# Hybrid S5 / RG-LRU / GLA block with ConvFFN: a new order for the first norm, the projection stream and one FFN operand, and a last scaling on VectorE with stores in two queues

## The chip, the cores and the metric

The kernel runs on one core of one Trainium2 chip. The metric is the device time of one execution in microseconds (us), the median of the runs. Engines are called PE (TensorE), DVE (VectorE), ACT (ScalarE), POOL (GpSimd) and SP (SyncE); PEld is the loading of weights into PE. Each engine works through its own queue in order. L12 is line 12 of the kernel's file.

## The reference, cut to what matters

One layer on 1024 latent tokens of width 1024, with a prefix of 256 context tokens. All of it is fp32.

```python
mod = split((silu(c) @ ada_w + ada_b), 6)
u  = rms_norm(h, ln1_g) * (1 + mod[1]) + mod[0]          # latent; uc likewise for the context
z  = u @ w_in                                            # 5408 columns: s5, lru x, lru gate, q, k, v, g, z, 3 gates
s5  = s5_branch(z);  lru = rglru_branch(z);  gla = gla_branch(z)
m   = sum(sigmoid(gate[i]) * (y[i] @ w_br[i]) for i in range(3))
h   = h + mod[2] * (m @ w_out)
u   = rms_norm(h, ln2_g) * (1 + mod[4]) + mod[3]
gate, val = split(dwconv3(u @ w_up), 2)                  # 2 x 2816 columns
h   = h + mod[5] * ((silu(gate) * val) @ w_down)
out = rms_norm(h, final_g)
```

## The kernel before

**Products.** Channels lie on the 128 partitions and tokens on the free axis. Each fp32 matrix is split into a high part (a cast on ACT, L220, tiles ending in h) and a low part (the rest, a subtraction on DVE or POOL, L221, tiles ending in l); a product is three matmuls, high by high, high by low, low by high. A matmul is 128x512 unless said otherwise.

**Start.** The list `START` is an order written out by hand for every engine; each entry calls one small step. `x` loads a tile of the input and `sq` squares it on ACT (L391), `sa` adds the squares (L395; on DVE, but on POOL for the three entries of `ONPOOL`), `rs`, `re`, `rp`, `rb`, `rc` make the norm's factor (sums by PE, an addition on DVE, a power on POOL, a broadcast by PE, a copy on ACT). `a` loads one of the 8 pieces of a row of `ada_w` (SP), `ar` multiplies the 8 pieces (L316, 64 matmuls), `at`, `ac`, `am` bring the row into columns (DVE copy, PE, three DVE operations L365 to L367). `un`, `u`, `ul` make the operand `u` (DVE L320, ACT L323, DVE), `g`, `gh`, `gl` load and split the first weights, `m1`, `m2` are the first products (PE L434, L435, L441). The second argument is the half of the tokens, except for `a`, `ar` and the others on `ada_w`, whose first argument is the row.

**Stream.** `proj_stream` is a generator that yields the rest of the input projection matmul by matmul; `fill(us)` draws from it until a budget is spent, at 0.216 us a matmul, and `F(name)` takes the budget from the table `FILL`. So PE works on the projection while the recurrent branches keep DVE and ACT busy. Its weights come in the order of the list `wsrc`, over SP, with two raw buffers (wr) and three buffers of split weights (wh, wl). Each block of 1024 tokens is 48 matmuls and ends in a copy or an activation on ACT; `out_rows` (L577 to 581) copies and stores a block, `v_steps` makes rows of v for the context (copy L746), `z_steps` the decay's input (L703 to 718, its psum bank mb the one that L746 empties). These run beside the RG-LRU (`L971` to `L1005`); S5 follows (L1164 to L1264), then its GLU, then the four GLA heads.

**GLA heads and the end of the stream.** For each head `decays`, `keys` and `rest` run on DVE and ACT (L1303 to L1339); `transposed` (PE L1347) transposes the decayed keys that `keys` has made (DVE L1323). Head 0 has the budget `gtr` ahead of it. At the end of head 3 `scaled` broadcasts the norm (PE L279), scales on DVE and stores to `yosp` through SP; what is left of the stream is drawn by `fill(1e9)`. Then the four stored outputs are read back (`yr`, two buffers, L1549), split into `y0h`, `y0l` to `y3h`, `y3l` (ACT L220, DVE L221), and multiplied with w_br (PE L290 to L292).

**FFN up.** The products run as a scheme with seven instead of eight block products: operands `T1` to `T4` and `B11`, `B21`, `B22`, each a high and a low part of four 128x512 tiles. For the first two pairs of columns, `q[0]` and `q[1]`, the operands are made at the same time, in an order written by hand (`norm_order`): `hi(t, k)` and `lo(t, k)` make the parts of operand t (5 is B22), `sub` the differences, `units` the products by T1, T2, T3, `p3` the product by B22 (the scheme's third product), `p4` that by T4. `z57` (L1688, L1689) adds two products on DVE and so frees a psum bank for `p4`. `nxt` is the third pair.

**The end.** `last_out` broadcasts the last norm by PE, copies it to SBUF on ACT (L2188), scales eight tiles, six on DVE from psum (L2193) and two on POOL from the copy (L2191), and stores each through SP (L2194). It runs for three stretches of tokens; the last is tokens 256 to 511.

Of the kernel before, what the change touches and what calls it, by code (L numbers as in the profile page):

```python
# [20 lines left out]
KT = 8  # L21
# [16 lines left out]
def _parts(v, bits, n):  # L38
    out = []
    for _ in range(n):  # L40
# [69 lines left out]
def tile_kernel(tc, I, out, dbg=None):  # L110
# [154 lines left out]
    def t0(shape, tag, bufs=1):  # L265
        return p0_.tile(list(shape), F32, name=nm("t0"), tag=tag, bufs=bufs)
# [41 lines left out]
        SY.dma_start(w, (I["ada01"][r] if r < 4 else I["ada25"][r - 4])[:, k * 512:(k + 1) * 512])  # L308
        ada.setdefault(r, []).append(w)

    def ada_rows(r, p):


        for k, w in enumerate(ada.pop(r)):
            for j in range(4):
                PE.matmul(p[32 * j:32 * j + 32], c32[:, k], w[:, j * 128:(j + 1) * 128],  # L316
                          start=(k == 0), stop=(k == KT - 1), skip_group_check=True)
# [13 lines left out]
    class Start:  # L331
# [65 lines left out]
        @staticmethod
        def rs(j):
# [1935 lines left out]
```

## Time and profile before

| | us |
|---|---|
| median of 3 runs | 1577.93 (1577.77 to 1577.96) |
| the profiled execution, its own time | 1578.69 |
| span of the profiled execution, first to last instruction | 1576.6 |
| busy in the span: PE, PEld, DVE, ACT, POOL | 1513.6, 1248.9, 1096.1, 772.3, 414.6 |

Mean granted TensorE clock 0.985 of full speed; DMA 126 GB/s on average. The stages on the span's clock: start 0 to 72, stream with RG-LRU 140 to 235, S5 to 475, GLU and heads to 745, merge of the branches to 815, w_out and norm to 917, FFN up to 1410, FFN down to 1565, last norm to 1576.6. The profile is read by its page (busy time of each engine), by the list of waits (what an engine waited for, summed by line), by windows (busy time of each engine in a stretch) and by the timeline (single instructions with start and duration, the idle time before one in square brackets with what ended it). A busy PE is not PE at its peak.

### The profile page before, as it was taken

The numbers are of one execution on the slowest core, as the hardware profiler recorded it, in microseconds if no ns is written. First come the engines' busy times: TensorE is split into PE (matmuls) and PEld (weight loads), VectorE is DVE, ScalarE is ACT, GpSimd is POOL, SyncE is SP. The second block draws the span as 40 slices with busy tenths as digits, with TensorE's granted clock in tenths as the row PEclk, the third lists the DMA queues.
The fourth block names the chain that finished last, engine by engine and source line by source line (L and its number), as shares of the span: only waits on it lengthen the run. The fifth ranks groups of instructions, "written<-read, shape, count | busy, mean of one in ns | idle before, by whom it ended". The sixth has DMA issues, their size and how long they took to land. (4 is left out here: it accounts for less than half of the span.)

```text
span 1576.6 us, 21571 instructions
## 1 busy us (share of the span) xinstructions
PE 1513.6 (96%) x8144; PEld 1248.9 (79%) x8144; DVE 1096.1 (70%) x1645; ACT 772.3 (49%) x1223; POOL 414.6 (26%) x266
## 2 busy tenths in 40 slices
PE   5999989999996999999999989999999999999997
PEld 4788768877885888888888867778888888878887
DVE  3624379999858434642451899888888888899962
ACT  4523776785534543441332565444444444544661
POOL 2313210011124222222236335333333333000032
PEclk9999999999998999999999999999999999999998
DMA  9764533332224244131574411222222223964303
GB/s 327 256 213 132 187 129 105 117 101 59 59 67 134 77 135 148 70 88 63 172 239 145 141 60 54 94 81 80 81 81 83 93 92 109 371 240 141 101 20 107
DMA packets 93865, 199.04 MB, mean 126 GB/s; under 512 B 13505, under 2 KB 34881, under 8 KB 93633
## 3 DMA queue, kind: packets, MB, share of 16 engines
q1 hardware_dynamic: 82048, 181.75, 34.3%
q10 hardware_dynamic: 11712, 15.91, 2.9%
q8 instruction: 64, 1.05, 0.3%
q14 instruction: 41, 0.33, 0.1%
HBM read 159.11 MB, written 38.52 MB: 125 GB/s over the span
## 5 line engine op out<-in xcount | busy, mean ns | idle before, releaser
L221 POOL TENSOR_TENSOR wl<-wr,wh 128x1024 fp32r<-128x1024 f32 (+1 forms) x78 | 164.2, 2105 | 477.1 <-ACT wh L220 432.8
L220 ACT CAST wh<-wr 128x1024 fp32r<-128x1024 f32 (+2 forms) x87 | 77.1, 891 | 146.2 <-issue 41.3
L221 POOL TENSOR_TENSOR wp<-tmp,wp 128x512 fp32r<-128x512 f32 x44 | 75.2, 1726 | 217.6 <-ACT wp L220 217.6
L534 PE MATMUL ma<-uh,wh 128*128 128x512 f32 x272 | 116.9, 430 | 0.7 <-ACT pt L809 0.7
L534 PE MATMUL mb<-uh,wh 128*128 128x512 f32 x272 | 106.7, 392 | 0.0
L536 PE MATMUL ma<-ul,wh 128*128 128x512 f32 x272 | 106.7, 392 | 0.0
L536 PE MATMUL mb<-ul,wh 128*128 128x512 f32 x272 | 106.7, 392 | 0.0
L538 PE MATMUL mb<-uh,wl 128*128 128x512 f32 x272 | 106.2, 391 | 0.0
L538 PE MATMUL ma<-uh,wl 128*128 128x512 f32 x272 | 105.9, 389 | 0.0
L220 ACT CAST wp<-tmp 128x512 fp32r<-128x512 f32 x78 | 46.5, 619 | 91.4 <-DVE tmp L1648 91.2
L1714 DVE SCALAR_TENSOR_TENSOR ca<-gv,vec,ca 128x1023 f32<-128x1023 f32 (+2 forms) x66 | 62.2, 967 | 23.8 <-ACT ca L1706 23.6
L220 ACT CAST wp<-hd 128x512 fp32r<-128x512 f32 x88 | 52.8, 618 | 49.4 <-PE bkd L2023 26.3
L220 ACT CAST wp<-wr 128x512 fp32r<-128x512 f32 x97 | 58.2, 620 | 32.5 <-DMA wr<-in_wdn_dram 17.1
L1717 DVE SCALAR_TENSOR_TENSOR ca<-gv,vec,ca 128x1023 f32<-128x1023 f32 (+2 forms) x66 | 71.1, 1100 | 0.1
L1378 DVE SCALAR_TENSOR_TENSOR gl<-gl,gl 128x128 f32<-128x128 f32 x72 | 31.2, 433 | 53.1 <-ACT gl L1376 35.6
L534 PEld LDWEIGHTS ma<-uh,wh 128*128 128x128 f32 x272 | 51.3, 189 | 15.4 <-issue 5.2
L221 DVE TENSOR_TENSOR wp<-hd,wp 128x512 fp32r<-128x512 f32 x88 | 60.8, 708 | 1.2 <-ACT wp L220 1.0
L538 PEld LDWEIGHTS ma<-uh,wl 128*128 128x128 f32 x272 | 51.2, 188 | 11.3
L536 PEld LDWEIGHTS ma<-ul,wh 128*128 128x128 f32 x272 | 51.2, 188 | 11.3
L536 PEld LDWEIGHTS mb<-ul,wh 128*128 128x128 f32 x272 | 51.2, 188 | 11.2
L538 PEld LDWEIGHTS mb<-uh,wl 128*128 128x128 f32 x272 | 51.1, 188 | 11.4
L534 PEld LDWEIGHTS mb<-uh,wh 128*128 128x128 f32 x272 | 51.4, 189 | 9.6 <-issue 1.4
(643 smaller groups left out, 4606.3 us busy)
## 6 DMA issues: line engine op xcount, KB each, us to landing
wa<-in_ada_dram SPq DMA_DIRECT2D x96, 256.0 KB
wr<-in_wup_dram SPq DMA_DIRECT2D x46, 512.0 KB
wr<-in_win_dram SPq DMA_DIRECT2D x40, 512.0 KB
wr<-in_wdn_dram SPq DMA_DIRECT2D x22, 512.0 KB
hd<-hid SPq DMA_DIRECT2D x22, 512.0 KB
hid<-ca SPq DMA_DIRECT2D x21, 512.0 KB
wr<-in_wout_dram SPq DMA_DIRECT2D x16, 512.0 KB
tmp<-in_wdn_dram SPq DMA_DIRECT2D x22, 256.0 KB
```

Of the source, the lines that this page charges most:

```text
L220: S.copy(h, src)
L221: lo.tensor_tensor(l, src, f32(h), OP.subtract)
L534: PE.matmul(p[j], h[:, kk], uh[j][:, k], start=f, stop=False)
L536: PE.matmul(p[j], h[:, kk], ul[j][:, k], start=False, stop=False)
L538: PE.matmul(p[j], l[:, kk], uh[j][:, k], start=False, stop=e)
L1378: self.last = V.scalar_tensor_tensor(Sd[:, step], Sd[:, step - 1], self.dec[:, step:step + 1], Sd[:, step], OP.mult, OP.add)
L1714: V.scalar_tensor_tensor(a[:, t0_ + 1:t0_ + 1 + n1], x[:, o:o + n1], fw[0], a[:, t0_ + 1:t0_ + 1 + n1], OP.mult, OP.add)
L1717: V.scalar_tensor_tensor(a[:, t0_ + c - 1:t0_ + n - 1], x[:, o + c:o + n], fw[2], a[:, t0_ + c - 1:t0_ + n - 1], OP.mult, OP.add)
```

## The change

```diff
+        'gtr0': [13.0],
         'gtr': [3.37, 4.7, 3.88, 4.43],
...
-ONPOOL = [('sq', 2, 1), ('sq', 4, 1), ('sq', 6, 1)]
...
-    def ada_rows(r, p):
+    def ada_rows(r, p, k0=0, k1=KT):
-        for k, w in enumerate(ada.pop(r)):
+        for k in range(k0, k1):
+            w = ada[r][k]
...
-        def ar(r):
-            ada_rows(r, psm[:, r * 128:(r + 1) * 128])
+        def ar(r, k0, k1):
+            ada_rows(r, psm[:, r * 128:(r + 1) * 128], k0, k1)
...
-                t = sqs[k, j] = t0([128, 512], "sq", 3)
+                t = sqs[k, j] = t0([128, 512], "sq" if k != 2 else "sqp", 3 if k != 2 else 1)
...
-            (G if ("sq", k, j) in ONPOOL else V).tensor_tensor(accs1[j], accs1[j], sqs[k, j], OP.add)
+            V.tensor_tensor(accs1[j], accs1[j], sqs[k, j], OP.add)
...
-        wsrc.extend([win[i] for i in (35, 36, 37, 0, 5, 6, 3, 4)] + vsrc)
+        wsrc.extend([win[i] for i in (35, 36, 37, 0, 5, 3, 4)] + vsrc + [win[6]])
...
-        for b in range(2):
-            yield from lat(lambda p: out_rows(p, qsp[b]))
+        yield from lat(lambda p: out_rows(p, qsp[0]))
         for b in range(2):
             yield from ctx(lambda p: out_rows([p], ksp[b]))
         yield from v_steps([0, 1])
+        yield from lat(lambda p: out_rows(p, qsp[1]))
         yield from z_steps()
...
         if h == 0:
+            F("gtr0")
             F("gtr")
...
     lo(2, 3)
+    hi(5, 2); hi(5, 3)
+    for k in range(4):
+        lo(5, k)
     units(3)
...
-    hi(5, 2); hi(5, 3)
     for k in range(4):
-        lo(5, k, G)
         sub(4, k)
...
     nxt.sums((7, 3))
+    q[1].p3()
     q[0].p4()
     q[0].gate()
     q[0].out()
-    q[1].p3()
     q[1].p4()
...
-        rs = pt()[:, :w_]
-        S.copy(rs, pr[:, :w_])
+        last = c0 == 256
+        if not last:
+            rs = pt()[:, :w_]
+            S.copy(rs, pr[:, :w_])
         for k in range(KT):
-            if k % 3 == 2:
+            if k % 3 == 2 and not last:
...
-            SY.dma_start(out[k * 128:(k + 1) * 128, c0:c1], hT[k][:, c0:c1])
+            (S if last and k % 2 else SY).dma_start(out[k * 128:(k + 1) * 128, c0:c1], hT[k][:, c0:c1])
```

The list `START` is replaced as a whole. `ar` takes a range of the 8 pieces now: in the new list a row's first six stand ahead of its last two, and for row 0 the first six stand ahead of `rb`. In the old list ACT's squares of the second half (`sq`) stand ahead of `u` of the first two tiles for tiles 0 to 6; in the new list only those of tiles 0 to 2 do. The second half's `rs` to `rc` follow later, and `m1(2, 0)` stands ahead of `m1(0, 1)`. The loads on SP keep their order. Two new steps, `sp` and `sf`, are defined and stand nowhere in the list.

What this moves is shown at three places. The first is PE at the start, from its first instruction. Before (over_d is the vector that sums, con the identity, wa a piece of `ada_w`):

```order
L285 MATMUL sm_125<-over_d,t_145 128x1 x4
L279 MATMUL sm_131<-con,t_179 128x128 x4
L316 MATMUL sm_126<-wa_186,c_97 32x128 x4
L316 MATMUL sm_126<-wa_188,c_97 32x128 x4
L316 MATMUL sm_126<-wa_190,c_97 32x128 x4
```

Now, from the fifth piece of row 0 to the first product:

```order
L317 MATMUL sm_126<-wa_187,c_97 32x128 x4
L317 MATMUL sm_126<-wa_189,c_97 32x128 x4
L279 MATMUL sm_131<-con,t_215 128x128 x4
L317 MATMUL sm_126<-wa_218,c_97 32x128 x4
L317 MATMUL sm_126<-wa_220,c_97 32x128 x4
L352 MATMUL sm_125<-con,t_253 128x8
L444 MATMUL ma_127<-uh_109,wh_133 128x512
L445 MATMUL ma_127<-uh_109,wl_134 128x512
```

The broadcast (L279) stood ahead of all eight pieces and stands now between the sixth and the seventh.

The second is SP's queue around the store of head 3 (`yosp`), where the third argument of a load tells its size. Before:

```order
L211 DMA wr_6774<-in_wbr_dram 128x256
L1434 DMA yosp<-gl_6512 128x1024
L211 DMA wr_6892<-in_wbr_dram 128x512
L1863 DMA acc_8093<-in_wup_dram 128x512
L1549 DMA yr_6904<-yosp 128x1024
L1549 DMA yr_6908<-yosp 128x1024
```

Now:

```order
L211 DMA wr_6759<-in_wbr_dram 128x256
L211 DMA wr_6892<-in_wbr_dram 128x512
L211 DMA wr_6898<-in_wbr_dram 128x512
L211 DMA wr_6951<-in_wbr_dram 128x512
L1444 DMA yosp<-gl_6596 128x1024
L1874 DMA acc_8093<-in_wup_dram 128x512
L1560 DMA yr_6904<-yosp 128x1024
L1560 DMA yr_6908<-yosp 128x1024
```

Three loads of w_br's third part, which came behind the store, stand ahead of it now. On PE, 66 matmuls of the stream are left behind head 3's broadcast where 126 were, and 60 more stand ahead of head 0's transposes.

The third is the low part of B22 in the FFN. Before, on POOL:

```order
L221 TENSOR_TENSOR wp_8212<-pt_7868,wp_8212 128x512
L221 TENSOR_TENSOR wp_8215<-acc_8093,wp_8215 128x512
L1837 TENSOR_TENSOR B22l<-h_7281,B22h 128x512
L1837 TENSOR_TENSOR B22l<-h_7283,B22h 128x512
L1837 TENSOR_TENSOR B22l<-h_7285,B22h 128x512
L1837 TENSOR_TENSOR B22l<-h_7287,B22h 128x512
```

Now, on DVE (L1659 are the sums of the third pair's weights, L221 the low parts of its first ones):

```order
L1848 TENSOR_TENSOR T2l<-h_7279,T2h 128x512
L1848 TENSOR_TENSOR B22l<-h_7281,B22h 128x512
L1848 TENSOR_TENSOR B22l<-h_7283,B22h 128x512
L1848 TENSOR_TENSOR B22l<-h_7285,B22h 128x512
L1848 TENSOR_TENSOR B22l<-h_7287,B22h 128x512
L1659 TENSOR_TENSOR tmp_8194<-wr_8099 128x512
L1659 TENSOR_TENSOR tmp_8196<-tmp_8194,wr_8097 128x512
L221 TENSOR_TENSOR wp_8198<-wr_8097,wp_8198 128x512
```

The four subtractions have left POOL and stand on DVE directly behind the last part of T2, ahead of the third pair's sums.

## Rows read from the trace of the kernel before

**Rows 1.** Page: busy us, share of the span, instructions of each engine.
```profile
PE 1513.6 (96%) x8144; PEld 1248.9 (79%) x8144; DVE 1096.1 (70%) x1645; ACT 772.3 (49%) x1223; POOL 414.6 (26%) x266
```

**Rows 2.** Waits of PE, whole span: us in total, times, longest us.
```profile
PE sm L1347 <- DVE gl L1323: 12.6, 1, 12.6
PE ma L434 <- ACT uh L323: 4.9, 1, 4.9
PE mb L711 <- ACT pt L746: 4.8, 1, 4.8
PE bkd L853 <- DVE gv L1688: 4.0, 2, 3.1
```

**Rows 3.** Windows: length, busy us of PE, PEld, DVE, ACT, POOL, PEclk, DMA share, GB/s.
```profile
20.00:40.00 20.00, 14.52 (x196) 12.06 (x187) 9.45 (x20) 6.95 (x14) 6.91 (x7) 0.83 0.91 323
210.00:220.00 10.00, 5.22 (x17) 2.83 (x15) 9.35 (x6) 7.82 (x10) 0.00 (x0) 0.66 0.40 131
220.00:230.00 10.00, 10.00 (x97) 6.34 (x96) 4.07 (x4) 9.46 (x10) 2.39 (x1) 0.99 0.17 55
350.00:360.00 10.00, 10.00 (x53) 8.03 (x52) 9.84 (x18) 7.04 (x13) 2.79 (x2) 1.00 0.32 96
510.00:520.00 10.00, 10.00 (x42) 8.52 (x42) 3.04 (x2) 2.02 (x4) 2.50 (x1) 0.82 0.21 67
```

**Rows 4.** Timeline of the start: start, us, engine, line, operation, out<-in, count.
```profile
17.85 3.64 PE L316 MATMUL sm<-wa,c 128*32 128x128 f32 x64
22.63 1.25 DVE L366 TENSOR_TENSOR mods<-mods,vec 128x4 f32<-128x4 f32 x1
26.50 1.32 ACT L323 ACTIVATE uh<-x,mods 128x512 fp32r<-128x512 f32 x2
35.23 3.66 SPq L308 DMA_DIRECT2D wa<-in_ada_dram  x8
```

**Rows 5.** Timeline of DVE at the end of the RG-LRU.
```profile
234.18 1.49 DVE L985 SCALAR_TENSOR_TENSOR lt<-lt,XC 128x1280 f32<-128x1280 f32 x1 [3.18 <-ACT lt L972]
```

**Rows 6.** Timeline of DVE ahead of head 0's transposes.
```profile
507.56 2.12 DVE L1323 TENSOR_TENSOR gl<-gl,gl 128x1280 f32<-128x1280 f32 x1 [2.73 <-ACT gl L1316]
```

**Rows 7.** Timeline of PE, SP and DVE around the end of head 3.
```profile
740.17 1.95 PE L279 MATMUL sm<-con,gl 128*128 128x128 f32 x16
...
743.35 0.40 PE L534 MATMUL ma<-uh,wh 128*128 128x512 f32 x1
743.58 0.39 PE L534 MATMUL mb<-uh,wh 128*128 128x512 f32 x1
...
744.71 0.33 SPq L1434 DMA_DIRECT2D yosp<-gl  x1
...
747.83 0.90 SPq L1549 DMA_DIRECT2D yr<-yosp  x2
...
755.67 0.32 SPq L1549 DMA_DIRECT2D yr<-yosp  x1
...
764.79 1.23 DVE L221 TENSOR_TENSOR y3l<-yr,y3h 128x1024 fp32r<-128x1024 f32 x1 [2.12 <-ACT y3h L220]
```

**Rows 8.** Timeline of POOL and DVE in the FFN's first pairs.
```profile
942.94 6.84 POOL L1837 TENSOR_TENSOR B22l<-h,B22h 128x512 fp32r<-128x512 f32 x4
...
945.15 1.78 DVE L1837 TENSOR_TENSOR T4l<-h,T4h 128x512 fp32r<-128x512 f32 x1
...
952.66 0.67 DVE L1688 TENSOR_TENSOR gv<-gv,bkd 128x512 f32<-128x512 f32 x1
```

**Rows 9.** Timeline of DVE and SP at the last scaling.
```profile
1569.52 2.08 DVE L2193 TENSOR_TENSOR h<-h,bkb 128x256 f32<-128x256 f32 x6 [2.27 <-ACT pt L2188]
...
1570.32 3.75 SPq L2194 DMA_DIRECT2D out_dram<-h  x8
```

**Rows 10.** Timeline of SP and DVE in head 1's loads of keys.
```profile
552.81 1.09 SPq L1322 DMA_DIRECT2D gl<-ksp  x2
...
559.04 1.49 DVE L1323 TENSOR_TENSOR gl<-gl,gl 128x1280 f32<-128x1280 f32 x1 [7.26 <-ACT tmp L1413]
```

More of the change, by code (lines that the diff above doesn't have):

```diff
@@ L85 @@
 ENGS = {mybir.EngineType.DVE, mybir.EngineType.Pool, mybir.EngineType.Activation, mybir.EngineType.SP}
-ONPOOL = [('sq', 2, 1), ('sq', 4, 1), ('sq', 6, 1)]
-START = [('x', 0, 0), ('sq', 0, 0), ('x', 1, 0), ('sq', 1, 0), ('x', 2, 0), ('sq', 2, 0), ('sa', 1, 0), ('x', 3, 0), ('sq', 3, 0), ('sa', 2, 0), ('x', 4, 0), ('sq', 4, 0), ('sa', 3, 0), ('x', 5, 0), ('sq', 5, 0), ('sa', 4, 0), ('x', 6, 0), ('sq', 6, 0), ('sa', 5, 0), ('x', 7, 0), ('sq', 7, 0), ('sa', 6, 0), ('sa', 7, 0), ('rs', 0), ('re', 0), ('rp', 0), ('rb', 0), ('a', 0, 0), ('a', 0, 1), ('a', 0, 2), ('a', 0, 3), ('a', 0, 4), ('a', 0, 5), ('a', 0, 6), ('a', 0, 7), ('g', 0), ('gh', 0, 0), ('gh', 0, 1), ('ar', 0), ('gl', 0, 0), ('rc', 0), ('gl', 0, 1), ('gh', 0, 2), ('x', 0, 1), ('sq', 0, 1), ('gl', 0, 2), ('x', 1, 1), ('sq', 1, 1), ('at', 0), ('ac', 0), ('x', 2, 1), ('sq', 2, 1), ('sa', 1, 1), ('x', 3, 1), ('sq', 3, 1), ('am', 0), ('sa', 2, 1), ('x', 4, 1), ('sq', 4, 1), ('un', 0, 0), ('x', 5, 1), ('sq', 5, 1), ('un', 1, 0), ('x', 6, 1), ('sq', 6, 1), ('u', 0, 0), ('sa', 3, 1), ('u', 1, 0), ('ul', 0, 0), ('m1', 0, 0), ('sa', 4, 1), ('x', 7, 1), ('sq', 7, 1), ('ul', 1, 0), ('sa', 5, 1), ('m2', 0, 0), ('m1', 1, 0), ('sa', 6, 1), ('sa', 7, 1), ('m2', 1, 0), ('rs', 1), ('a', 1, 0), ('a', 1, 1), ('a', 1, 2), ('a', 1, 3), ('a', 1, 4), ('a', 1, 5), ('a', 1, 6), ('a', 1, 7), ('g', 1), ('gh', 1, 0), ('ar', 1), ('re', 1), ('gh', 1, 1), ('rp', 1), ('gh', 1, 2), ('gl', 1, 0), ('rb', 1), ('at', 1), ('gl', 1, 1), ('gl', 1, 2), ('ac', 1), ('rc', 1), ('am', 1), ('un', 0, 1), ('un', 1, 1), ('u', 0, 1), ('a', 2, 0), ('a', 2, 1), ('a', 2, 2), ('a', 2, 3), ('a', 2, 4), ('a', 2, 5), ('a', 2, 6), ('a', 2, 7), ('ar', 2), ('un', 2, 0), ('u', 1, 1), ('ul', 0, 1), ('g', 2), ('gh', 2, 0), ('u', 2, 0), ('gl', 2, 0), ('m1', 0, 1), ('ul', 1, 1), ('gh', 2, 1), ('gh', 2, 2), ('at', 2), ('gl', 2, 1), ('ul', 2, 0), ('ac', 2), ('gl', 2, 2), ('un', 3, 0), ('m2', 0, 1), ('m1', 1, 1), ('am', 2), ('u', 3, 0), ('un', 2, 1), ('ul', 3, 0), ('m1', 2, 0), ('u', 2, 1), ('un', 3, 1), ('a', 3, 0), ('a', 3, 1), ('a', 3, 2), ('a', 3, 3), ('a', 3, 4), ('a', 3, 5), ('a', 3, 6), ('a', 3, 7), ('ar', 3), ('ul', 2, 1), ('u', 3, 1), ('un', 4, 0), ('g', 3), ('gh', 3, 0), ('gh', 3, 1), ('gl', 3, 0), ('ul', 3, 1), ('gh', 3, 2), ('m2', 1, 1), ('u', 4, 0), ('gl', 3, 1), ('at', 3), ('un', 5, 0), ('m2', 2, 0), ('gl', 3, 2), ('ul', 4, 0), ('ac', 3), ('u', 5, 0), ('m1', 3, 0), ('am', 3), ('ul', 5, 0), ('m1', 2, 1), ('un', 4, 1), ('un', 5, 1), ('u', 4, 1), ('m2', 3, 0), ('un', 6, 0), ('u', 5, 1), ('m2', 2, 1), ('ul', 4, 1), ('u', 6, 0), ('m1', 3, 1), ('ul', 5, 1), ('ul', 6, 0), ('m1', 4, 0), ('un', 7, 0), ('un', 6, 1), ('m2', 3, 1), ('u', 7, 0), ('un', 7, 1), ('m2', 4, 0), ('u', 6, 1), ('ul', 7, 0), ('m1', 5, 0), ('u', 7, 1), ('ul', 6, 1), ('m1', 4, 1), ('ul', 7, 1), ('m2', 5, 0), ('m2', 4, 1), ('m1', 5, 1), ('m1', 6, 0), ('m2', 5, 1), ('m2', 6, 0), ('m1', 6, 1), ('m2', 6, 1), ('mz',)]
@@ new lines @@
+START = [('x', 0, 0), ('sq', 0, 0), ('x', 1, 0), ('sq', 1, 0), ('x', 2, 0), ('sq', 2, 0), ('sa', 1, 0), ('x', 3, 0), ('sq', 3, 0), ('sa', 2, 0), ('x', 4, 0), ('sq', 4, 0), ('sa', 3, 0), ('x', 5, 0), ('sq', 5, 0), ('sa', 4, 0), ('x', 6, 0), ('sq', 6, 0), ('sa', 5, 0), ('x', 7, 0), ('sq', 7, 0), ('sa', 6, 0), ('sa', 7, 0), ('rs', 0), ('a', 0, 0), ('a', 0, 1), ('a', 0, 2), ('a', 0, 3), ('a', 0, 4), ('a', 0, 5), ('ar', 0, 0, 6), ('re', 0), ('rp', 0), ('a', 0, 6), ('a', 0, 7), ('g', 0), ('gh', 0, 0), ('rb', 0), ('gh', 0, 1), ('gl', 0, 0), ('gh', 0, 2), ('x', 0, 1), ('sq', 0, 1), ('gl', 0, 1), ('x', 1, 1), ('sq', 1, 1), ('gl', 0, 2), ('ar', 0, 6, 8), ('rc', 0), ('sa', 1, 1), ('x', 2, 1), ('sq', 2, 1), ('at', 0), ('ac', 0), ('sa', 2, 1), ('am', 0), ('un', 0, 0), ('un', 1, 0), ('u', 0, 0), ('u', 1, 0), ('ul', 0, 0), ('m1', 0, 0), ('ul', 1, 0), ('x', 3, 1), ('sq', 3, 1), ('x', 4, 1), ('sq', 4, 1), ('sa', 3, 1), ('m2', 0, 0), ('x', 5, 1), ('sq', 5, 1), ('m1', 1, 0), ('sa', 4, 1), ('x', 6, 1), ('sq', 6, 1), ('sa', 5, 1), ('x', 7, 1), ('sq', 7, 1), ('a', 1, 0), ('a', 1, 1), ('a', 1, 2), ('a', 1, 3), ('a', 1, 4), ('a', 1, 5), ('ar', 1, 0, 6), ('sa', 6, 1), ('sa', 7, 1), ('m2', 1, 0), ('a', 1, 6), ('a', 1, 7), ('g', 1), ('gh', 1, 0), ('gh', 1, 1), ('gl', 1, 0), ('ar', 1, 6, 8), ('gh', 1, 2), ('rs', 1), ('at', 1), ('gl', 1, 1), ('gl', 1, 2), ('ac', 1), ('re', 1), ('rp', 1), ('am', 1), ('a', 2, 0), ('a', 2, 1), ('a', 2, 2), ('a', 2, 3), ('a', 2, 4), ('a', 2, 5), ('ar', 2, 0, 6), ('un', 2, 0), ('un', 3, 0), ('u', 2, 0), ('rb', 1), ('u', 3, 0), ('ul', 2, 0), ('a', 2, 6), ('a', 2, 7), ('g', 2), ('gh', 2, 0), ('ul', 3, 0), ('gh', 2, 1), ('gl', 2, 0), ('gh', 2, 2), ('ar', 2, 6, 8), ('rc', 1), ('gl', 2, 1), ('m1', 2, 0), ('at', 2), ('un', 0, 1), ('gl', 2, 2), ('un', 1, 1), ('u', 0, 1), ('ac', 2), ('m2', 2, 0), ('un', 2, 1), ('u', 1, 1), ('a', 3, 0), ('a', 3, 1), ('a', 3, 2), ('a', 3, 3), ('a', 3, 4), ('a', 3, 5), ('ar', 3, 0, 6), ('am', 2), ('u', 2, 1), ('ul', 0, 1), ('m1', 0, 1), ('ul', 1, 1), ('ul', 2, 1), ('a', 3, 6), ('a', 3, 7), ('g', 3), ('gh', 3, 0), ('gh', 3, 1), ('ar', 3, 6, 8), ('gl', 3, 0), ('un', 3, 1), ('gh', 3, 2), ('m2', 0, 1), ('gl', 3, 1), ('at', 3), ('u', 3, 1), ('un', 4, 0), ('m1', 1, 1), ('gl', 3, 2), ('ul', 3, 1), ('u', 4, 0), ('ac', 3), ('un', 5, 0), ('m2', 1, 1), ('am', 3), ('u', 5, 0), ('m1', 3, 0), ('ul', 4, 0), ('ul', 5, 0), ('m1', 2, 1), ('un', 4, 1), ('un', 5, 1), ('u', 4, 1), ('m2', 3, 0), ('un', 6, 0), ('u', 5, 1), ('m2', 2, 1), ('ul', 4, 1), ('u', 6, 0), ('m1', 3, 1), ('ul', 5, 1), ('ul', 6, 0), ('m1', 4, 0), ('un', 7, 0), ('m2', 3, 1), ('un', 6, 1), ('u', 7, 0), ('m2', 4, 0), ('un', 7, 1), ('u', 6, 1), ('m1', 5, 0), ('ul', 7, 0), ('u', 7, 1), ('ul', 6, 1), ('m1', 4, 1), ('ul', 7, 1), ('m2', 5, 0), ('m2', 4, 1), ('m1', 5, 1), ('m1', 6, 0), ('m2', 5, 1), ('m2', 6, 0), ('m1', 6, 1), ('m2', 6, 1), ('mz',)]
@@ L394, in sa, with sp, sf @@
         def sa(k, j):
-            (G if ("sq", k, j) in ONPOOL else V).tensor_tensor(accs1[j], accs1[j], sqs[k, j], OP.add)
+            V.tensor_tensor(accs1[j], accs1[j], sqs[k, j], OP.add)
+        @staticmethod
+        def sp(k, j):
+            G.tensor_tensor(sqs[2, j], sqs[2, j], sqs[k, j], OP.add)
+        @staticmethod
+        def sf(j):
+            Start.sa(2, j)
         @staticmethod
```

## The prediction

> **What bounds the kernel now.** I read the page first, then the list of PE's waits, then windows and timelines at the longest waits. PE is busy for 1513.6 of the span's 1576.6 us [rows 1], and the profiled execution's own time is 1578.69, so no edit off PE's path can bring more than about 63 us, and these edits leave the number of matmuls as it is. What can be gained is PE's waiting, and the slow matmuls behind a wait. Four of the waits lie where the change works: 12.6 us ahead of head 0's transposes, 4.9 at the first product, 4.8 in the decay's input, 4.0 in two waits on z57 [rows 2]. Behind each the granted clock is low for a while. Its two levels are 1.2 and 2.4 GHz, so a mean of 0.83 over 20 us is 2 x 0.17 x 20 = 6.8 us at the lower one, 0.66 over 10 us the same, and 0.82 over 10 us is 3.6 us [rows 3]. Work that runs in such a stretch takes twice as long. A wait is worth its length and half of the busy slow time behind it, but only if the engine that ends it is not simply late further on.
>
> **1. Start.** The first product waits for `u` on ACT, which begins at 26.50 [rows 4]. In front of it three things go. The multiplication by the norm's gain in the row's conversion (L366), of only 4 elements a partition, took 1.25 us [rows 4], while one of 512 elements takes 0.67 [rows 8]; a POOL addition ran beside it, and that addition moves to DVE: at least 0.6 back. From its end at 23.88, `u` needs one scaling of 512 elements (0.7) and could begin near 24.6 instead of 26.50, since the squares that stood in ACT's queue ahead of it stand behind it now: 1.9. And 48 of the row's 64 matmuls (2.7 of 3.64 us, [rows 4]) go ahead of the broadcast, into time in which PE waited for POOL's power: some 1.5 of that is idle time used. Together 4.0. The squares and additions of the second half are late next. They feed products that come some 15 us later, and DVE must take 3 more additions of 0.67 for it: if these stand in the way, 4.0 - 2.0 = 2.0 is left. If instead the slow stretch also goes, in which PE was busy for some 5.2 us, it is 4.0 + 2.6 = 6.6. `ar` of row 1 runs earlier too, so the loads that wait for its buffers at 35.23 [rows 4] start earlier; nothing else on SP is moved. I take **4.0 (2.0 to 6.6)**.
>
> **2. Order of the stream.** The wait of 4.8 is for ACT's copy of a v row [rows 2], which stands in ACT's queue behind RG-LRU work. Now 48 matmuls (11.0 us, at the pitch of 0.23 in [rows 7]) come between the v rows and the decay's input, so the bank is long empty. With the slow 4.3 us behind it (busy 5.22 of 10 at a mean of 0.66, [rows 3]), that is 4.8 + 2.2 = 7.0 on PE. But PE does not set the end there: ACT is busy 9.46 of 10 us in the next window, and S5 begins when ACT's last gate lets DVE start at 234.18 [rows 5], and from then on DVE is full, 9.84 of 10 at 350 [rows 3]. Only what moves that start counts. Below: nothing, if ACT's chain alone sets it. The gates wait for PE's products too, which come up to 4.8 earlier, and the row is nearer to the chain on ACT, whose window is full to 95%, so I take a little under half, **3.0 (0 to 7.0)**.
>
> **3. The fill ahead of head 0.** Its budget is 13.0 at 0.216 a matmul; the step that crosses it is finished, so 10 steps of 6, 60 matmuls. At a pitch of 0.23 [rows 7] they take 13.8 us, in a wait of 12.6 that ends when DVE has made the keys at 507.56 + 2.12 [rows 6]. The transposes then come 1.2 later and run, with what follows, at full clock: the slow 3.6 us in the window [rows 3] give back 1.8. In all 13.8 - 1.2 + 1.8 = 14.4. The work is taken from the stream's end. There 126 matmuls cover 29 us from the broadcast's end at 742.1; 66 cover 15.2, to 757.3. Under that cover runs a chain: scaling, store at 744.71, read back from 747.83, a third read at 755.67 when a buffer comes free, the last low part at 764.79 + 1.23 = 766.0 [rows 7]. Nobody waited for it; now somebody does. The store also stands behind three loads, the third of which needs a raw buffer that is free once the block ahead is split, some 4 us after the broadcast: about 1.2 later than now. The first product of 24 matmuls would end at 757.3 + 5.5 = 762.8 without a wait; its last operand comes at 766.0 + 1.2, so it ends near 767.7 (its last two matmuls behind that), a wait of 4.9. The two late reads share the queue with less than before, since the loads that came among them have gone ahead, so I take 4. Bounds: none, if the reads are that much faster, and 4.9 + 3.4 (half of 6.8 us at the low clock) = 8.3. Net **10.4 (6.1 to 14.4)**.
>
> **4. B22 in the FFN.** On POOL the four subtractions take 6.84 us, and four DVE operations beside them take 1.78 instead of 0.67 [rows 8]. On DVE they cost 4 x 0.67 = 2.7 and give back 4 x 1.11 = 4.4: z57 at 952.66 [rows 8] comes 1.7 earlier, and PE, which waits 4.0 there in two waits [rows 2], has `q[1].p3` (12 matmuls, 2.8 us) to do first. So PE's wait can go whole, 4.0; but what DVE saves, on which the pairs behind depend, is 1.7 and not more; and if the third pair's sums, 2.7 later now, hold up its first weights, it is nothing. I take **2.5 (0 to 4.0)**: DVE's 1.7 and a third of the rest. POOL gets idle time, which costs nothing.
>
> **5. The tail.** The copy on ACT (0.4) goes, and the first scaling can start as soon as the broadcast is there. Eight scalings on DVE at 2.08 / 6 = 0.35 end after 2.8 us. SP issued eight stores in 3.75 us, one per 0.47 [rows 9], later than DVE could feed them; two queues of four take 1.9, so DVE sets the pace. The last store goes out near 1572.0 instead of 1573.6, and this is worth 1.6, and the copy shortens the start. If the transfers are the limit, they end no sooner than 1.05 MB at 323 GB/s [rows 3] = 3.3 us after the first: then 0.4 + 0.3 = 0.7. I take **1.7 (0.7 to 2.1)**. The Trainium skill, page "DMA: Bandwidth & Descriptors", section "Issuing engines are not separate DMA queues", speaks against the second queue: transfers from all engines share the same 16 DMA engines, and only the time to issue is saved, which is usually small. By it the term would be the lower bound, if issuing is small; in the row the issuing of eight stores takes 3.75 us and is all of the tail.
>
> **The sum.** 4.0 + 3.0 + 10.4 + 2.5 + 1.7 = 21.6. Against the profiled execution that is 1578.69 - 21.6 = 1557.1; the median of the runs shown stands 0.76 below it, so the forecast is 1577.93 - 21.6 = 1556.3, **1556 us**. Chance 0.55.
>
> **Rivals.**
> - *Every wait counts whole*: the reads keep up, and S5 and the FFN start with PE: 4.0 + 7.0 + 14.4 + 4.0 + 1.7 = 31.1, **1546.8**. For it: the kernel's long waits all lie on PE. Against: DVE full in S5. Chance 0.13.
> - *DVE keeps its dates*: terms 2 and 4 give nothing and the start 2.0: 2.0 + 10.4 + 1.7 = 14.1, **1563.8**. For it: DVE's 9.84 of 10 at 350 [rows 3]. Chance 0.22.
> - *The store waits for the stream*: if the third load in front of `yosp` gets its buffer only when the stream's last products are done, at 757.3, the chain of 766.0 - 744.71 = 21.3 us begins there. Less the 4 us of products that can run meanwhile, and with 3.4 of slow clock, it takes 20.7 from the 14.4: 4.0 + 3.0 - 6.3 + 2.5 + 1.7 = 4.9, **1573.0**. Against: the block it needs ends right behind the broadcast. Chance 0.04.
> - *Nothing is left*: S5's DVE swallows terms 1 and 2, and the exposed chain most of 3: some 2 us, **1576**, no change. Chance 0.03.
> - *Slower: a head's keys behind a weight load.* SP's queue holds loads of weights ahead of each head's loads. Head 1's keys were issued at 552.81, behind such loads, and DVE used them at 559.04 [rows 10]; 6.2 less 3.1 for a transfer (as long as `yosp` takes from issue to the reads behind it, [rows 7]) leaves 3.1 us of slack. Should the load in front wait for one block more (48 matmuls, 11.0 us), each of heads 1 to 3 comes 7.9 late, and with a slow stretch behind each (half of 6.8) that is 3 x 11.3 = 33.9 against the 21.6 gained: **1590**. It decides from 21.6 / 3 = 7.2 a head on. Against it: the load in front is one block further on in the stream's list, but the stream is 60 matmuls, 1.25 blocks, further too. Chance 0.03.
>
> **The numbers.** About 0.2%, 3.2 us, is what a measurement of this kernel can tell from no change. Forecast and the first three rivals are faster by more: 0.55 + 0.13 + 0.22 + 0.04 = 0.94; same 0.03; slower 0.03. The range runs from the case where all waits count (1546) to the low ends of terms 2 to 4 together, 1577.93 - (4.0 + 0 + 6.1 + 0 + 1.7) = 1566.1, so **1546 to 1567**; it leaves out the last three rivals and what lies above it in the third.
>
> **What would show it.** Right: the first product near 23.2; no wait of the decay's input on ACT's copy of v; no wait of PE ahead of head 0's transposes over 1 us and a clock near 1 behind it; a new wait of 2 to 6 us in the first products of w_br's third part (L290 to 292) for a `y2` or `y3` part; z57's wait under 1 us; stores over within 5 us of the last broadcast. Wrong: a wait moved from the decay's input to S5's first product of the same size (term 2 gone), a wait on head 1's keys (the slower rival), or a wait at L290 over 10 us (the store behind the stream).

## The result, and the profile after

The changed kernel takes 1551.38 us (1549.47 to 1552.56, 4 runs) beside 1577.95 for the kernel before in the same rounds (1577.77 to 1578.85): a ratio of 0.9829, with a 95% interval of 0.9812 to 0.9846. A second series gave 1550.28 beside 1578.14, 0.9825 (0.9811 to 0.9838). The forecast of 1556 (1546 to 1567, faster) holds; the gain is 26.6 us where 21.6 was worked out. The time lies as near to the first rival (1546.8) as to the forecast.

The busy times on the page, which answer [rows 1]: PE's share of the span is a point higher, POOL has less to do by 16 us, and DVE has nine operations more and is not busier for it.

```profile
PE 1508.9 (97%) x8144; PEld 1242.9 (80%) x8144; DVE 1090.4 (70%) x1654; ACT 772.1 (50%) x1222; POOL 398.1 (26%) x257
```

The waits of PE in the whole span (us in total, times, longest), which answer [rows 2]:

```profile
PE sm L285 <- DVE sp L922: 12.0, 1, 12.0
PE ma L444 <- ACT uh L324: 2.0, 1, 2.0
...
PE bkd L863 <- DVE gv L1699: 1.5, 1, 1.5
...
PE bkc L863 <- ACT gv L1695: 0.9, 1, 0.9
...
PE mm L291 <- DVE y2l L221: 0.8, 1, 0.8
...
PE mm L290 <- ACT y2h L220: 0.6, 1, 0.6
...
PE mm L291 <- DVE y3l L221: 0.5, 1, 0.5
```

The waits of 12.6 and 4.8 have left the list, the first product waits 2.0 where it waited 4.9, and three short waits for the read-back heads (`mm`, `y2`, `y3`), 2.0 together, are new. Of the two waits on z57's operation, 4.0 before, the one of 3.1 is gone. The 1.5 that is left (`bkd`) is ended by a matmul of a later pair, at 990.08, as the other wait, of 0.9, was before (1034.95); so the sign "under 1 us" came true only for the first pairs. The windows that answer [rows 3], with the heads' window at its new place (same columns):

```profile
20.00:40.00 20.00, 17.41 (x217) 13.49 (x217) 13.53 (x27) 9.17 (x18) 5.70 (x7) 0.83 1.05 387
210.00:220.00 10.00, 9.50 (x97) 6.30 (x96) 5.83 (x6) 9.62 (x14) 2.40 (x1) 1.00 0.18 59
490.00:500.00 10.00, 10.00 (x46) 8.23 (x45) 7.25 (x5) 5.69 (x10) 5.40 (x4) 1.00 0.01 2
500.00:510.00 10.00, 10.00 (x59) 8.27 (x59) 2.74 (x1) 4.56 (x9) 7.39 (x3) 1.00 0.53 176
```

In the RG-LRU and at head 0 the clock is at 1.00 and PE at 9.5 to 10 of 10. In the start the mean clock is 0.83 as before: the wait became shorter, the slow stretch did not.

Where the time went is read from the dates at which the same instructions (for a wait, the wait itself) start in both traces. A line's share is what it adds to the line above.

| landmark | before | after | earlier by | share of the stage |
|---|---|---|---|---|
| first stream matmul | 72.48 | 68.56 | 3.9 | start 3.9 |
| S5's first output product | 342.64 | 331.69 | 10.9 | order of the stream 7.0 |
| last matmul of the stream | 770.55 | 744.93 | 25.6 | fill at head 0, 14.7 |
| PE's first wait in the FFN | 916.71 | 893.94 | 22.8 | given back behind the stream, -2.9 |
| PE's wait at the start of FFN down | 1409.91 | 1384.30 | 25.6 | FFN 2.8 |
| the profiled execution's own time | 1578.69 | 1550.97 | 27.7 | FFN down and tail 2.1 |

These are single executions. PE's first instruction, ahead of which the two lists of the start are the same, starts at 12.66 before and at 12.01 after, and between 11.7 and 12.8 in the other kernels' traces, so some 0.6 of the first line is not the change's. By the spans, 1576.6 and 1549.2, the last line is 1.8.

### The profile page after: what moved, and what is told of

The parts are those of the page before. It is cut to its first block, busy times and chain, and to the rows that moved or that the text cites. A ratio compares the mean times of both kernels' runs of the same rounds, so it can differ in the third digit from the quotient of the medians.

```text
span 1549.2 us, 21566 instructions
## 1 busy us (share of the span) xinstructions
PE 1508.9 (97%) x8144; PEld 1242.9 (80%) x8144; DVE 1090.4 (70%) x1654; ACT 772.1 (50%) x1222; POOL 398.1 (26%) x257
## 3 DMA queue, kind: packets, MB, share of 16 engines
q8 instruction: 64, 1.05, 0.3%
## 5 line engine op out<-in xcount | busy, mean ns | idle before, releaser
L221 POOL TENSOR_TENSOR wl<-wr,wh 128x1024 fp32r<-128x1024 f32 (+1 forms) x78 | 161.1, 2067 | 450.5 <-ACT wh L220 426.8
L221 POOL TENSOR_TENSOR wp<-tmp,wp 128x512 fp32r<-128x512 f32 x44 | 73.6, 1692 | 211.6 <-ACT wp L220 200.9
L1725 DVE SCALAR_TENSOR_TENSOR ca<-gv,vec,ca 128x512 f32<-128x512 f32 (+2 forms) x66 | 61.0, 949 | 25.4 <-ACT ca L1717 25.0
L1728 DVE SCALAR_TENSOR_TENSOR ca<-gv,vec,ca 128x1023 f32<-128x1023 f32 (+2 forms) x66 | 69.6, 1080 | 0.1
L221 DVE TENSOR_TENSOR wp<-hd,wp 128x512 fp32r<-128x512 f32 x88 | 60.9, 710 | 0.9 <-ACT wp L220 0.8
```

The costliest lines, as they stand in the source:

```text
L221: lo.tensor_tensor(l, src, f32(h), OP.subtract)
L1725: V.scalar_tensor_tensor(a[:, t0_ + 1:t0_ + 1 + n1], x[:, o:o + n1], fw[0], a[:, t0_ + 1:t0_ + 1 + n1], OP.mult, OP.add)
L1728: V.scalar_tensor_tensor(a[:, t0_ + c - 1:t0_ + n - 1], x[:, o + c:o + n], fw[2], a[:, t0_ + c - 1:t0_ + n - 1], OP.mult, OP.add)
```

## The experiments

Kernels of one series share the runs of the kernel before (medians 1577.65, 1578.14 and 1578.32 in the three series). The changed kernel ran beside the others in the second series only, 1550.28; its first runs gave 1551.38. Differences below are between medians, against 1551.38 for the first series and 1550.28 for the other two. Single runs of the change lie up to 3 us apart, those of the run without the new start 6.6. So parts of 1 to 3 us are read from dates in the traces too. The five parts, each undone alone, add up to 30.0 by the medians, 3.4 more than the whole gain. All line numbers of after and of the experiments are some 10 higher than before.

**Start undone.**
```diff
+ONPOOL = [('sq', 2, 1), ('sq', 4, 1), ('sq', 6, 1)]
...
-            V.tensor_tensor(accs1[j], accs1[j], sqs[k, j], OP.add)
+            (G if ("sq", k, j) in ONPOOL else V).tensor_tensor(accs1[j], accs1[j], sqs[k, j], OP.add)
...
-        def ar(r, k0, k1):
+        def ar(r):
```
and the old list.

> The start's list, its three additions on POOL and the undivided ada rows as before, all else as in the change. Theory (PE sets the pace from the start to the end, so what the start gives arrives whole): the first stream matmul, at 68.56 with the change, comes at 72.5, and the time is 3.9 us above the changed kernel's 1551.4, near 1555.3. Rival (S5 runs at DVE's pace and swallows it): the first stream matmul is late all the same, but S5's first output product (331.7 with the change) moves by less than 1 us and the time by less than 1.

Measured 1555.13 (1552.01 to 1558.65), 3.8 above. The wait at the first product is back:

```profile
PE ma L445 <- ACT uh L325: 4.7, 1, 4.7
```

In the profiled execution, the fastest of the four, the first stream matmul comes at 71.03, where 72.5 was expected, and S5's first output product at 333.61: 2.5 and 1.9 later than with the change. The size is less sure than the sign, but S5 does not swallow it. In this run L366's operation takes 0.16 as with the change, and the two scalings behind it, beside which POOL's addition now falls, take 2.31 where they take 1.42 with the change.

**Order of the stream undone.**
```diff
-        wsrc.extend([win[i] for i in (35, 36, 37, 0, 5, 3, 4)] + vsrc + [win[6]])
+        wsrc.extend([win[i] for i in (35, 36, 37, 0, 5, 6, 3, 4)] + vsrc)
...
-        yield from lat(lambda p: out_rows(p, qsp[0]))
+        for b in range(2):
+            yield from lat(lambda p: out_rows(p, qsp[b]))
...
-        yield from lat(lambda p: out_rows(p, qsp[1]))
```

> The stream's old order (both q blocks ahead of the context's k blocks), all else as in the change. Theory (PE's wait and its slow clock count whole): PE waits near 4.8 us for ACT's copy of v again, the clock is low for some 5 us behind it, S5's first output product moves from 331.7 to about 338.7, and the time is 7.0 above 1551.4, near 1558.4. Rival, that of the prediction (ACT's and DVE's chain sets S5's start, so only part counts): the wait is back, but the time rises by 3.0 or less, to 1554.4 at most.

Measured 1559.49 (1556.53 to 1560.97), 8.1 above; S5's first output product comes at 339.26, 7.6 later. The theory holds and the prediction's rival, 3.0 or less, falls. PE's wait is that of before, and so is the mean clock of the window, 0.66. A wait of this run, then its window:

```profile
PE mb L721 <- ACT pt L756: 4.8, 1, 4.8
```
```profile
210.00:220.00 10.00, 8.30 (x73) 5.23 (x77) 5.63 (x5) 7.01 (x10) 1.61 (x1) 0.66 0.36 122
```

Why it counts whole is seen in whom PE waits for behind it. From the end of this wait to S5's first output product PE waits for nobody, neither before (216.5 to 343) nor in this run (213 to 340); with the change there is one wait of 0.5 between 200 and 332. PE's own queue is full there, so what PE loses moves S5's product by all of it. DVE does not hold PE further on either: PE's waits for DVE in S5 are the same before, with the change and in this run, whose row reads as the second.

```profile
PE sm L1260 <- DVE s L1245: 1.7, 2, 1.3
```
```profile
PE sm L1270 <- DVE s L1255: 1.7, 2, 1.3
```

DVE's chain came forward with PE. Its operation of [rows 5], at 234.18 before, starts at 230.65 in this run and at 221.00 with the change:

```profile
221.00 1.49 DVE L995 SCALAR_TENSOR_TENSOR lt<-lt,XC 128x1280 f32<-128x1280 f32 x1 [0.58 <-ACT lt L982]
```

One link by which it hangs on PE shows in ACT's waits. ACT's gates waited for PE's gate products, and those lay behind the stalled decay's input in PE's queue. This wait, before (190 to 250) and in this run (180 to 250), is gone with the change:

```profile
ACT lt L972 <- PE sm L971: 2.6, 1, 2.6
```
```profile
ACT lt L982 <- PE sm L981: 3.0, 2, 2.8
```

ACT's full window was no sign of the bound: with the change ACT is as full from 210 to 220 (9.62 of 10) as it was from 220 to 230 before (9.46).

**Fill undone.**
```diff
-        'gtr0': [13.0],
...
-            F("gtr0")
```

> Without the new budget ahead of head 0, all else as in the change. Theory (14.5 won at head 0, 2.9 of it given back at the stream's end): PE waits 12 to 13 us ahead of head 0's transposes, the three waits for y2 and y3 parts are gone, and the time is 11.7 above 1551.4, near 1563.1. Rival (the chain at the stream's end would be waited for in any case): waits of 2 us for y2 and y3 stay and the time is 14.5 above, near 1566.

Measured 1564.03 (1563.27 to 1564.93), 12.7 above. The wait at head 0 is back, and there is none for a `y` part in its list:

```profile
PE sm L1356 <- DVE gl L1332: 12.7, 1, 12.7
PE ma L543 <- ACT pt L818: 0.8, 1, 0.8
PE ma L825 <- DVE acc L836: 0.5, 1, 0.5
```

So the waits behind the stream are the price of the fill, and the net is about 12. The rival falls.

**FFN part undone, twice.**
```diff
-    hi(5, 2); hi(5, 3)
-    for k in range(4):
-        lo(5, k)
     units(3)
...
+    hi(5, 2); hi(5, 3)
     for k in range(4):
+        lo(5, k, G)
...
-    q[1].p3()
     q[0].p4()
...
+    q[1].p3()
     q[1].p4()
```

> B22's low part on POOL and the old place of q[1].p3, all else as in the change. Theory (PE's wait on z57 counts, less what the pairs behind give back): a wait near 3.1 us on z57 is back, with a low clock behind it, and the time is 2.9 above 1551.4, near 1554.3. Rival (DVE sets the pace of these pairs, and saves 1.7): the wait is back but the time rises by 1.7 or less.

Measured 1552.77 (1552.69 to 1556.02), 1.4 above: it fits the rival by the median, but the series holds no second run of the changed kernel. So again, with five rounds, beside it:

> The changed kernel itself, again, as the reference for the small parts. Every theory: 1551.4, between 1549.5 and 1552.6 as its first runs.

> The FFN part undone once more (B22's low part on POOL, old place of q[1].p3), beside the changed kernel in the same rounds. Theory (PE's 3.1 us on z57 and its slow clock count, 2.9): 1554.3 where the changed kernel shows 1551.4. Rival (DVE's 1.7 is all): 1553.1 or less.

Measured 1550.28 (1549.67 to 1551.74) and 1553.33 (1552.65 to 1553.64), 3.1 above, with no overlap. All runs together, eight of each kernel, put the medians 2.3 apart. The dates are steadier: from PE's first wait in the FFN to its wait at the start of FFN down it is 490.4 and 490.6 in the two profiles of the change, 493.2 before, and 494.9 and 493.1 in the two runs with the part undone. So the theory, 2.9, holds against 1.7 or less. z57's waits in the second run, of which the longest is that of the first pairs:

```profile
PE bkd L863 <- DVE gv L1699: 3.9, 2, 3.1
```

**Only the third product's place undone.**
```diff
-    q[1].p3()
     q[0].p4()
...
+    q[1].p3()
     q[1].p4()
```

> B22's low part on DVE as in the change, but q[1].p3 back behind the output of q[0]. Theory (the earlier third product only fills PE's time until z57): PE waits some 1 to 2.5 us on z57 again and the time is 1 to 2 above the changed kernel. Rival (the operand's move is the whole of it): z57 comes in time, no new wait over 1 us, and the time is within 0.5 of it.

Measured 1551.62 (1550.70 to 1552.82), 1.3 above, but the runs overlap with those of the changed kernel. The trace shows a wait of 1.2 on z57 and a longer one for weights behind it, which is 1.2 with the change in the same series:

```profile
PE bkb L864 <- DVE wp L221: 2.4, 1, 2.4
PE bkd L863 <- DVE gv L1699: 2.0, 2, 1.2
```

The waits are the theory's, but the dates settle it for the rival: the stretch of the FFN named above is 490.3 here, no longer than with the change. The operand's move is the whole gain; what PE waits for z57 without the earlier product it does not lose over the stretch.

**Tail undone, and its second queue alone undone.**
```diff
-        last = c0 == 256
-        if not last:
-            rs = pt()[:, :w_]
-            S.copy(rs, pr[:, :w_])
+        rs = pt()[:, :w_]
+        S.copy(rs, pr[:, :w_])
...
-            (S if last and k % 2 else SY).dma_start(out[k * 128:(k + 1) * 128, c0:c1], hT[k][:, c0:c1])
+            SY.dma_start(out[k * 128:(k + 1) * 128, c0:c1], hT[k][:, c0:c1])
```
In the first run POOL scales two of the eight tiles again. The second run has the last pair of these lines alone.

> The last scaling and its stores as before, all else as in the change. Theory (the tail is worth 1.7): from the last broadcast's start to the end of the span 8.5 us instead of 6.8, time 1.7 above the changed kernel. Rival (the transfers set the end, the issuing is hidden): 0.7 or less above it.

> The change with all last stores issued by SP again; the scaling stays on DVE alone. Theory (the second queue is the larger part of the tail's gain, since one queue issues a store per 0.47 us and DVE feeds one per 0.35): from the last broadcast's start to the end near 7.9 us instead of 6.8 to 7.3, transfers near 265 GB/s instead of 340, time 1.0 above the changed kernel. Rival (the Trainium skill's rule taken at its word: the DMA engines are the limit, issuing is small): no more than 0.3 above it, at the same rate of transfer.

Measured 1552.69 (1551.55 to 1553.66) and 1552.93 (1552.23 to 1554.05), 2.4 and 2.7 above, in two series. The medians can't be the tail alone: the smaller edit would cost as much as the larger, which holds it. From DVE's first scaling to the end of the span it is 7.6 us with the tail undone, 6.8 with one queue, and 6.1 and 6.0 in the two profiles of the change: about 0.7 for each half, or 1.5 together. In the kernel before it is 7.1, by which the two halves are worth 1.0. ACT's copy (0.4), which ends ahead of the first scaling, comes on top. Part of the 2.7 is not the tail's: the run with one queue has a stretch of low clock at 750 to 760 (last section). The theory on the queue holds in direction and in rate. The DMA view of the last 8 us (from 1544 on) with one queue, share and GB/s in 40 slices, and then of the last 7 us with two:

```profile
DMA  0000000000496896968959598695970000000000
GB/s 0 41 0 0 0 0 0 0 0 0 133 343 205 297 287 200 343 195 302 292 190 348 180 328 277 215 348 164 338 256 5 0 0 0 0 0 0 0 0 0
```
```profile
DMA  0000000089999999999999999800000000000000
GB/s 0 0 0 0 0 0 0 6 263 363 310 357 322 351 345 340 328 369 310 351 345 328 357 328 339 269 12 0 0 0 0 0 0 0 0 0 0 0 0 0
```

With one queue the engines run dry between two stores; with two they are full at some 340 GB/s, and the transfer is the limit. The Trainium skill, page "DMA: Bandwidth & Descriptors", section "Issuing engines are not separate DMA queues", says that a second issuing engine saves only the time to issue, usually small; the trace agrees that nothing else is saved, and here issuing (8 stores in 3.75 us, [rows 9]) was longer than the transfer (1.05 MB at 340 GB/s, 3.1 us).

**Four buffers for the read-back, and the store on ACT.**
```diff
-        t = pyp.tile([128, 1024], F32, name=nm(name), tag=name, bufs=2)
+        t = pyp.tile([128, 1024], F32, name=nm(name), tag=name, bufs=4 if name == "yr" else 2)
...
-            (SY if self.h == 3 else S).dma_start(yosp[self.h], og)
+            S.dma_start(yosp[self.h], og)
```
The first run has the first pair alone, the second both.

> The change with four buffers in place of two for the read-back of the four heads, so that the third and fourth read need not wait for the first to be split. Theory (the 2 us of waits at the stream's end come from the two buffers): the third read is issued near 736 instead of 744, the waits of PE for y2 and y3 parts go, time 2.0 below the changed kernel, near 1549. Rival (the transfers themselves are the limit): the four reads and the two behind them share the engines, y0 or y1 comes later, a wait of about 2 us stands at the first product instead, time within 0.5 of the changed kernel.

> As the run with four buffers, and head 3's store is issued by ACT, as the other heads' are, and not by SP behind three loads. Theory (the store goes out when DVE has scaled, 733.8 in the profile of the change, and SP was not late): issue within 0.3 us of the run before, time within 0.5 of it. Rival, the prediction's (the third load in front holds the store for 1.2): the store goes out 1 us earlier.

Measured 1550.88 (1549.21 to 1552.13) and 1548.75 (1547.75 to 1549.77), where the change gave 1550.28 in the series before. With four buffers, the four reads go out together:

```profile
733.32 0.33 SPq L1444 DMA_DIRECT2D yosp<-gl  x1
...
734.17 3.61 SPq L1560 DMA_DIRECT2D yr<-yosp  x4
```

One wait for a `y` part is left of three, 1.1 us in the first run and 0.5 in the second, so most of these waits do come from the two buffers. What that is worth in time is not shown. PE's first wait in the FFN begins at 892.01 and 891.55 instead of 893.94, but the stream's last matmul is 0.5 and 0.3 earlier already. From there to that wait it is 147.6 and 146.9, and in the nine profiles with two buffers and the fill of 13.0 it is anything from 147.4 to 150.1. By the times the first run is within noise of the change and the second is the lowest median of all kernels here, a ratio of 0.9815 (0.9802 to 0.9828) that overlaps with the change's 0.9825; it lies 2.1 below the first run, where 0.5 was expected, and their runs overlap. The store on ACT goes out at 733.50, no sooner than SP's, and in both runs 0.03 behind the end of DVE's last multiplication, so the prediction's 1.2 us behind three loads falls. What made it later than before is seen in the trace of the change, in that multiplication, SP's store and the third read:

```profile
732.12 1.67 DVE L1443 TENSOR_TENSOR gl<-gl,acc 128x512 f32<-128x512 f32 x1
```
```profile
733.82 0.33 SPq L1444 DMA_DIRECT2D yosp<-gl  x1
...
744.06 1.56 SPq L1560 DMA_DIRECT2D yr<-yosp  x2
```

The multiplication took 1.67, two and a half times the 0.67 of [rows 8], and ends at 733.79; the store follows at once. From the start of head 3's broadcast to the store it is 5.5 where it was 4.5. POOL's split of a weight starts just ahead of the multiplication here, at 731.95; before, it started behind it (744.26; the multiplication, at 744.00, took 0.68). That this made it slow, as in [rows 8], was not tried apart.

**A smaller fill.**
```diff
-        'gtr0': [13.0],
+        'gtr0': [10.0],
```

> The budget ahead of head 0 is 10.0 in place of 13.0, so 8 steps of 6 matmuls instead of 10. Theory (the fill only has to cover head 0's keys, and what it takes is missed at the stream's end): a wait of 1.7 us ahead of head 0's transposes (12.65 less 48 matmuls at 0.2275), the waits at the stream's end gone, time within 1 of the changed kernel. Rival (the waits at the stream's end don't come from the cover): a wait of 1.7 at head 0, the same 2 us at the end, time 1.7 above it.

Measured 1558.54 (1555.80 to 1560.23), 8.3 above. Both expectations fall. The wait at head 0 is 2.0 where 1.7 was expected, and the waits behind the stream shrink to 0.5, but a wait of a kind that is hardly there with the change (0.2) comes twice, once in head 2 and once in head 3. Waits of PE from 480 to 770, then ACT at the first of them, then PE there:

```profile
PE ma L544 <- ACT pt L819: 4.4, 2, 2.5
PE sm L1357 <- DVE gl L1333: 2.0, 1, 2.0
PE mm L291 <- DVE y3l L221: 0.5, 1, 0.5
```
```profile
636.47 1.04 ACT L1392 COPY gl<-gl 64x1024 f32<-64x1024 f32 x1 [3.20 <-DVE gl L1388]
637.52 1.04 ACT L1391 COPY gl<-gl 64x1024 f32<-64x1024 f32 x1
638.59 0.60 ACT L819 ACTIVATE pt<-ma 128x512 f32<-128x512 f32 x1
```
```profile
639.24 0.66 PE L544 MATMUL ma<-uh,wh 128*128 128x512 f32 x1 [2.46 <-ACT pt L819]
```

The block's activation, which empties PE's bank, stands in ACT's queue behind two copies of a head's states that wait for DVE. The clock is low after the wait at head 0 and after each of the two new ones:

```profile
500.00:510.00 10.00, 10.00 (x61) 8.16 (x62) 1.91 (x1) 3.83 (x8) 5.07 (x3) 0.86 0.46 170
...
640.00:650.00 10.00, 10.00 (x51) 8.56 (x52) 6.34 (x8) 3.69 (x8) 3.57 (x2) 0.86 0.19 67
...
700.00:710.00 10.00, 9.94 (x47) 8.24 (x48) 2.58 (x4) 1.74 (x4) 3.10 (x2) 0.83 0.19 66
```

By the dates the stream's last matmul comes 8.3 later than with the change (753.23) and PE's first wait in the FFN 6.3 (900.21). The FFN up, where nothing was edited, took 2.5 longer in this execution, with a clock of 0.83 from 900 to 920, so some 6 us are the smaller fill's.

With 48 matmuls ahead of head 0 instead of 60, the ends of the stream's blocks fall on other places in the heads. In this part of the stream a gated block is 48 matmuls and 12 of w_br, 60 in all, so a fill of 60 leaves the ends where they were, and one of 48 does not. That this is why 13.0 does no harm was argued, not tried with further sizes.

## Why the prediction was right

Sign and range were right, and four of the five terms came within 1.5 us of the dates; the sum was 5 to 6 short, and 4 of that lie in the one term whose mechanism was wrong. The range held the result because it reached down to the rival in which every wait counts whole.

- **Start, 4.0 forecast, 3.9 by the dates, 3.8 by the medians of the run that undoes it and 2.5 by its date.** The first product starts at 22.59, 0.6 ahead of the 23.2 named. Counted from PE's first instruction, ACT's `u` comes 4.0 earlier: 1.1 from the row, where 1.5 was forecast (an addition of DVE stands ahead of the row's copy in the new list, and PE waits 1.5 for the copy), 1.2 from L366, which takes 0.16 now (0.6 forecast), and 1.8 from the squares (1.9). The sum is right in part because two errors cancel, and 0.8 of it is lost again by the first stream matmul. The clock is as low as before, so the upper bound of 6.6 had no share in it.
- **Order of the stream, 3.0 forecast, 7.0 and 8.1 measured: the step that failed.** The prediction took the window full of ACT (9.46 of 10) and DVE's full S5 as what sets S5's start, "nearer to the chain on ACT". The run that undoes it shows PE full and waiting for nobody from that wait to S5's first output product, which moves by all of it; ACT's gates wait 3.0 us for PE there, and DVE's start moves with PE. The price of 7.0, the wait and half of the slow time behind it, stood there as the upper bound, and was the right one.
- **Fill, 10.4 forecast, 11.8 by the dates, 12.7 by the run.** Gross 14.4 forecast, 14.7 measured. What is given back was put at 4 and is 2.9: the waits for the `y` parts are 2.0 together where 4.9 stood as the working's own result. The chain from the store to the last low part became shorter, 18.4 us (733.82 to 752.20) where it was 21.3. The store is 1.0 later against the broadcast, where 1.2 was forecast, but that is luck: the cause given, the loads in front of it, was wrong; the store waited for DVE.
- **FFN, 2.5 forecast, 2.8 and 3.1 measured.** z57 comes 2.0 earlier against the FFN's first wait (1.7 forecast), and PE, in place of waiting 3.1, does the third product and waits 0.9 within it for its bank and 0.3 for its weights. The prediction read the waits of 4.0 as one place; 0.9 of them lay in a later pair. That the third product's place adds a share was wrong: with the old place the stretch is as long.
- **Tail, 1.7 forecast, 1.8 by the dates within the span, 1.4 to 1.9 by the stretch from the first scaling on and the copy.** The transfers are the limit now; DVE, which the prediction named, ends first. So the size was right with another limit than the one it was worked out from; for this limit the prediction had 0.7.
- **Rivals.** "Every wait counts whole" named the right price for the stream and too much for the fill; "DVE keeps its dates" falls with the second run. The store did not wait for the stream. The slower rival, a head's keys behind a weight load, shows nowhere in the waits of the change. Its relative did show in the smaller fill: another queue (ACT's), and some 6 us.

## What to carry to other kernels

A full engine beside a stalled one is not yet the bound: look for whom the stalled engine waits for next. Here PE waited for nobody for over 100 us behind its stall, so all that it lost there was lost at the end, however full ACT and DVE were. A filler placed in a wait has three prices: the wait it covers, the cover that is missed where it was taken from, and the places at which its blocks now end; the last cost some 6 us here, more than the second. A fill of one whole period of the blocks did not meet it here; that the period is the reason was not tried. Stores at the end that follow each other faster than one queue issues them gained from a second queue, up to where the DMA engines were full.

## What the runs showed of the hardware that was not expected

The lower clock comes in some executions and not in others after the same short waits. One kernel's profile (one queue for the last stores) has it behind waits of 2.0 us for the `y` parts, and the profile of the change, with the same 2.0, has not. Nor is it the length of the waits alone: the first run with the FFN part undone has it behind waits of 1.5 (window also 0.83), the run with the third product's old place, with 2.1, has it not (1.00). The window from 750 to 760 in the run with one queue and in the change:

```profile
750.00:760.00 10.00, 9.57 (x36) 7.75 (x37) 5.34 (x6) 2.77 (x4) 1.30 (x1) 0.83 0.31 97
```
```profile
750.00:760.00 10.00, 9.42 (x40) 7.43 (x41) 5.75 (x6) 3.33 (x5) 1.57 (x2) 1.00 0.38 107
```

A mean of 0.83 over 10 us is 3.4 us at the lower level, so some 1.7 us of work lost (an estimate, as PE was busy nearly all of it). That is more than half of the 3 us by which single runs of the changed kernel differ, and it is why parts of this size are better told from dates and from waits than from a few medians.
